# Ending a convolution's last channel block by halves of the tokens, with a norm per half, ahead of a projection in an inference kernel

## The chip, the cores and the metric

The kernel runs on one core of one Trainium2 chip. The metric is the device time of one execution in microseconds (us). The engines named below are PE (TensorE, matrix products), DVE (VectorE), ACT (ScalarE), POOL (GpSimd) and SP (its queue issues the weight loads). Each engine works through its own instructions in the order in which they are written, and waits where one needs something that another engine has not delivered.

## The reference, cut to what matters

Two transformer-like blocks are chained on 512 tokens of 1024 channels. The part that matters is the convolution mixer of the second block, followed by its output projection:

```python
def conformer_conv(h, w_pw1, dw_w, dw_b, ln_g, ln_b, w_pw2):
    a, g = jnp.split(h @ w_pw1, 2, axis=-1)
    u = a * jax.nn.sigmoid(g)
    u = causal_dwconv(u, dw_w, dw_b)          # 31 taps, each channel alone
    u = jax.nn.silu(layer_norm(u, ln_g, ln_b)) # mean and variance over the 1024 channels of a token
    return u @ w_pw2
```

The layer norm needs, for each token, the sum and the sum of squares over all 1024 channels. So nothing of `silu(...)`, and nothing of the projection by `w_pw2`, can start for a token before the convolution of the last channel is done for this token.

## The kernel before, in words

Activations lie with channels on the 128 partitions and the 512 tokens along the free dimension. 1024 channels are 8 blocks (KB = 8), numbered 0 to 7. float32 products are made of three fp32r products: each operand is cut into a high part (names that end in h, or `whi`) and a low part (l, or `wlo`), and high x high, high x low and low x high are added in PSUM.

The order of the work is written out by hand. The program issues instructions engine by engine in the order of the Python code, and waits between engines follow from the tiles that they share. The weights come through one stream `W` in a fixed order: an SP load into a `stage` buffer, an ACT cast to `whi` (line 96), and a DVE subtraction to `wlo` (line 106). Six cut chunks are held, and a slot comes free when PE is done with the chunk in it.

In the convolution stage, for each channel block i, two products of `w_pw1` give `a` and `g`, and `glu` makes u (tile `cu`, with its parts `cuh` and `cul`). The 31 taps are then shared out:
- PE does the first `n_pe[i]` taps as products with a diagonal matrix (`taps`, lines 1628 to 1630, into the PSUM tile `ps_dw`). ACT makes the diagonals `dh` and `dl` (lines 1602 and 1603). A product with the identity adds `pivot`, a rough mean that is taken off for precision (line 1632).
- POOL adds the next `n_pool[i]` taps up in `po`, where ACT does the multiplications.
- DVE does the rest (line 1643), adds the parts, and writes the block's result `y[i]` (lines 1647 to 1649 in `dwconv`).

Two running sums over the blocks (`n1` of y, `n2` of y squared, tiles `acc`) are added up by POOL, and the last but one block's by DVE. ACT makes the squares (tile `term`, line 319), DVE or POOL adds them (line 315). The last block is not added: its y and its square go to the sums over channels as they are.

The sum over channels is a PE product with a column of ones, one column of output per 128 tokens. Such a product appears as two records of shape 128x1 in the trace (in the class `Total`, line 352, tile `ps_ss`; in the class `HalfTotals`, which an earlier stage of the kernel uses, lines 388 and 403, tile `ps_hs`). Then DVE works a chain of some 14 tiny instructions on a few columns, which ends in the reciprocal square root (tile `ry`) and minus the mean times it (`lm`). PE transposes both so that they stand along the tokens on every partition (`turned`, line 443, tile `ps_bc`).

Before the projection each y block is normalised by DVE (lines 1727 and 1728, tile `lt`), put through Silu by ACT and cut into parts (`s0h`, `s0l` and so on). `lead_blocks` runs the first 4 output blocks of the projection abreast (lines 502, 503, 505 and 477 to 479), so that PE has 12 products for each input block as it arrives. The other 4 output blocks follow one at a time, 24 products each (`in_block`). Then the feed-forward part `ffn(1)` starts. Between the small steps `warm(n, ...)` issues products whose result nobody reads (line 458, tile `ps_w`). `S.activation(touch, touch, AF.Silu)` makes ACT load its table for Silu ahead of need.

Of the kernel before, what the change touches and what calls it, by code (L numbers as in the profile page):

```python
# [8 lines left out]
F32 = mybir.dt.float32  # L9
F32R = mybir.dt.float32r  # L10
I32 = mybir.dt.int32
AF = mybir.ActivationFunctionType
# [110 lines left out]
def fused(ctx: ExitStack, tc: tile.TileContext, a, out: bass.AP):  # L123
# [1422 lines left out]
    N_DIAG = 14  # L1546
    n_pe, n_pool = [9] * 6 + [11, 18], [8] * 7 + [7]
# [29 lines left out]
    def glu(i, pa, pg, rb):  # L1577
# [14 lines left out]
        u, w = tap(i, n_pe[i] + n_pool[i])  # L1592
        o2s[i] = bank("o2")
        S.activation(o2s[i], u, AF.Copy, scale=w)
# [22 lines left out]
    def taps(i, k0=0, k1=CW, between=None):  # L1617

        _, uh, ul = cu[i]
        if k0 == 0:  # L1620
            ps_dw[i] = bank("ps_dw")
        ps, n, res = ps_dw[i], n_pe[i], None
        for k in range(k0, min(k1, n)):
            if between and k == k0 + 1:
                res = between()
# [4 lines left out]
            PE.matmul(ps, dl, uh[:, s], start=False, stop=(i < 2 and k == n - 1))  # L1630
        if i > 1 and k1 >= n:
            PE.matmul(ps, identr, pivot, start=False, stop=True)
        return res

    def dwconv(i, k0=0, k1=CW):
# [5 lines left out]
        for m, k in list(enumerate(rest[:-1]))[k0:k1]:  # L1641
            t = ps if m % 2 and i < KB - 1 else o2
            V.scalar_tensor_tensor(t, *tap(i, k), t, op0=ALU.mult, op1=ALU.add)
        if k1 < CW:
            return
# [8 lines left out]
        if 1 < i < KB - 1:  # L1654
            ln_sums(i - 1)
        if i == KB - 1:
            ln_sums(i)


    def ln_sums(i):  # L1660
        last = i == KB - 1
        n1.plain(y[i], last=last)
        n2.square(y[i], last=last)
# [10 lines left out]
    for i in range(KB):  # L1674
# [21 lines left out]
    def begin_sums():  # L1696
        return [Total(n).begin().copy() for n in (n1, n2)]
# [7 lines left out]
    nm = small.tile([P, NT], F32, tag="lm", name="lm")  # L1705
    V.tensor_scalar(nm, s1, -1.0 / D, None, op0=ALU.mult)
    sq = small.tile([P, NT], F32, tag="lq", name="lq")
    V.tensor_scalar(sq, s2, 1.0 / D, EPS, op0=ALU.mult, op1=ALU.add)
    var = small.tile([P, NT], F32, tag="lv", name="lv")
    V.tensor_mul(var, nm, nm)  # L1710
    V.scalar_tensor_tensor(var, var, -1.0, sq, op0=ALU.mult, op1=ALU.add)
# [12 lines left out]
    def ln_a(i):  # L1724
        if i < KB:
            t = work("lt")
            V.tensor_mul(t, y[i], rb)
            V.tensor_add(t, t, nb)
            sl[i] = part_pair(f"s{i}", slp, "sl")
            if i == 0:  # L1730
                S.activation(sl[i][0], t, AF.Silu, bias=col("ln_b", i), scale=col("ln_g", i))
            S.activation(t, t, AF.Silu, bias=col("ln_b", i), scale=col("ln_g", i))
            if i > 0:
                S.copy(sl[i][0], t)
            cur[i] = t

    def ln_b(i):
        ln_a(i + 1)
        return second_part(sl[i], cur.pop(i))

    lead = 4
    ln_a(0)
    pss = lead_blocks(ln_b, lead)
# [104 lines left out]
```

## Time and profile before

| what | us |
|---|---|
| median of 3 runs (lowest, highest) | 1699.74 (1699.52, 1700.22) |
| the profiled execution's own time | 1698.82 |
| span of its trace | 1696.5 |
| PE busy, by the page | 1684.5 |
| first product of the projection by `w_pw2` starts at | 1288.64 |
| first product of `ffn(1)` starts at | 1332.28 |

Times in the trace count from the start of the span. The profiled execution took 2.3 us more than its span, and 0.92 us less than the median of the runs. A busy time counts the length of the records; PE's records overlap, because one product enters the array before the one ahead has left it. So the pace of PE is read from the distance between starts and not from the length of a record.

### The profile page before, as it was taken

The page shows a single profiled execution, that of the slowest core. Times are in us where ns is not written, and L with a number is a line of the kernel's source. Part 1 is how long each engine was busy: PE and PEld are TensorE (multiplying, and loading weights), DVE is VectorE, ACT ScalarE, POOL GpSimd, SP SyncE. Part 2 cuts the span into 40 slices and gives each one's busy share as a digit, 9 for nine tenths or more (in the row PEclk, how much of TensorE's full clock was granted, in tenths as well). Part 3 has the DMA queues.
Part 4 walks back from the last instruction along what each step waited for, and adds up shares of the span by engine and source line. Part 5 has one row for each costly group of instructions (what it writes and reads, how often), then busy time and mean ns, then how long its engine had stood idle before and what let it go on. Part 6 is the DMA issues. An engine that isn't in the chain of part 4 may idle for free.

```text
span 1696.5 us, 20684 instructions
## 1 busy us (share of the span) xinstructions
PE 1684.5 (99%) x7950; PEld 1409.8 (83%) x7950; DVE 1089.1 (64%) x1780; ACT 754.6 (44%) x1237; POOL 109.5 (6%) x104
## 2 busy tenths in 40 slices
PE   9999999999999999999999999999999999999999
PEld 7888898888888987888888888888887888888887
DVE  8877866244346876765874377557987487636752
ACT  4433453333233345863543244457885254323430
POOL 0000000000000000000000000006880000000000
PEclk8999999999999999999999999999999999999999
DMA  9477315332324132112333332232210223333332
GB/s 355 151 235 237 100 60 167 109 96 86 119 66 121 48 107 88 51 32 68 101 95 92 110 100 84 87 115 88 74 51 17 83 88 110 93 109 100 91 99 71
DMA packets 53667, 176.12 MB, mean 104 GB/s; under 512 B 6081, under 2 KB 6337, under 8 KB 52674
## 3 DMA queue, kind: packets, MB, share of 16 engines
q1 hardware_dynamic: 53570, 174.82, 32.0%
q8 instruction: 62, 1.02, 0.3%
q14 instruction: 35, 0.29, 0.1%
HBM read 172.69 MB, written 2.10 MB: 103 GB/s over the span
## 4 chain that ended last, share of the span: by engine, by line
PE 95%; DVE 2%; ACT 1%; issue 0%; DMA 0%; SPq 0%; ACTq 0%; DVEq 0%
PE ps L477 25%; PE ps L478 25%; PE ps L479 25%; PE ps L621 2%; PE ps L1121 1%; PE ps L1123 1%; PE ps L1122 1%; PE ps L502 1%; PE ps L503 1%; PE ps L505 1%; PE ps_dw L1628 1%; PE ps_dw L1629 1%; PE ps_dw L1630 1%; PE ps_ss L352 1%; PE ps L915 1%; PE ps L912 1%
## 5 line engine op out<-in xcount | busy, mean ns | idle before, releaser
L106 DVE TENSOR_TENSOR wlo<-stage,whi 128x1024 fp32r<-128x1024 f32 (+3 forms) x312 | 336.2, 1104 | 82.2 <-ACT whi L96 81.1
L96 ACT CAST whi<-stage 128x1024 fp32r<-128x1024 f32 (+3 forms) x312 | 288.4, 950 | 178.4 <-DMA stage<-in_down 50.4
L1482 ACT ACTIVATE zo<-z,par 128x512 f32<-128x512 f32 x88 | 70.4, 814 | 156.6 <-DVE z L1480 156.5
L1486 DVE SCALAR_TENSOR_TENSOR zo<-z,par,zo 128x510 f32<-128x510 f32 (+1 forms) x176 | 123.4, 746 | 11.0 <-ACT zo L1482 11.0
L1480 DVE TENSOR_TENSOR z<-ps,rbc 128x512 f32<-128x512 f32 x88 | 59.2, 686 | 72.5 <-PE ps L479 69.0
L1575 POOL TENSOR_TENSOR po<-po,pr 128x512 f32<-128x512 f32 x55 | 73.0, 1328 | 18.2 <-ACT pr L1574 14.5
L545 DVE SCALAR_TENSOR_TENSOR ada<-ada,cs 128x1024 f32<-128x1024 f32 x48 | 58.3, 1218 | 7.8 <-DMA ada<-in_ada 7.7
L1489 ACT ACTIVATE zo<-zo 128x512 f32<-128x512 f32 x44 | 27.9, 633 | 66.2 <-DVE zo L1486 66.2
L1527 DVE TENSOR_TENSOR x<-x,ps 128x512 f32<-128x512 f32 x16 | 11.0, 688 | 67.1 <-PE ps L479 67.1
L932 DVE TENSOR_TENSOR r<-r 128x512 f32<-128x512 f32 x32 | 22.1, 690 | 46.6 <-ACT r L930 46.6
L315 DVE TENSOR_TENSOR acc<-acc,term 128x512 f32<-128x512 f32 (+1 forms) x68 | 44.2, 664 | 7.0 <-ACT term L319 5.8
L930 ACT ACTIVATE r<-ps 128x512 f32<-128x512 f32 x32 | 19.0, 595 | 60.4 <-PE ps L479 56.7
L963 DVE TENSOR_TENSOR y<-y,ps 128x512 f32<-128x512 f32 x14 | 9.6, 687 | 48.8 <-PE ps L479 48.8
L477 PE MATMUL ps<-n7h,whi 128*128 128x512 f32 x104 | 40.7, 391 | 0.0
L479 PE MATMUL ps<-n7h,wlo 128*128 128x512 f32 x104 | 40.5, 389 | 0.0
L478 PE MATMUL ps<-n7l,whi 128*128 128x512 f32 x104 | 40.5, 389 | 0.0
L1574 ACT ACTIVATE pr<-cu,par 128x512 f32<-128x512 f32 x55 | 39.0, 713 | 2.8 <-POOL po L1575 2.8
L1416 DVE TENSOR_TENSOR x<-x,ps 128x512 f32<-128x512 f32 x24 | 16.4, 684 | 35.3 <-PE ps L479 35.3
L477 PE MATMUL ps<-n0h,whi 128*128 128x512 f32 x96 | 38.1, 397 | 0.0
L1244 POOL MEMSET qk<- 128x8 f32 x4 | 0.5, 113 | 580.8 <-DVE mt L561 580.8
L477 PE MATMUL ps<-n1h,whi 128*128 128x512 f32 x96 | 37.4, 390 | 0.0
L479 PE MATMUL ps<-n0h,wlo 128*128 128x512 f32 x96 | 37.4, 389 | 0.0
(1382 smaller groups left out, 4973.0 us busy)
## 6 DMA issues: line engine op xcount, KB each, us to landing
stage<-in_up SPq DMA_DIRECT2D x88, 512.0 KB, 3.8
ada<-in_ada SPq DMA_DIRECT2D x34, 512.0 KB, 4.6
stage<-in_mlp_in SPq DMA_DIRECT2D x32, 512.0 KB, 3.9
stage<-in_down SPq DMA_DIRECT2D x32, 384.0 KB, 3.2
stage<-in_pw SPq DMA_DIRECT2D x24, 512.0 KB, 3.8
stage<-in_down SPq DMA_DIRECT2D x32, 320.0 KB, 3.4
stage<-in_mlp_out SPq DMA_DIRECT2D x28, 320.0 KB, 3.3
stage<-in_sc_in SPq DMA_DIRECT2D x16, 512.0 KB, 3.8
```

What stands on the lines that cost most here:

```text
L96: nc.scalar.copy(hi[:, :w], t[:, :w])
L106: self.nc.vector.tensor_sub(lo, t, hi)
L315: self.engine.tensor_add(self.acc[:, s], self.acc[:, s], t)
L477: PE.matmul(ps, hi, act[0], start=first, stop=False)
L478: PE.matmul(ps, hi, act[1], start=False, stop=False)
L479: PE.matmul(ps, lo, act[0], start=False, stop=last)
L545: V.scalar_tensor_tensor(t[:, s], t[:, s], 1.0, cs[:, s], op0=ALU.mult, op1=ALU.mult, accum_out=to)
L1480: V.tensor_mul(z, ps, rb)
L1482: S.activation(o, z, AF.Identity, bias=col(fcb, j), scale=col(fcw, 2 * 2 * FB + j))
L1486: V.scalar_tensor_tensor(o[:, s:], z[:, :T - s], col(fcw, (2 - s) * 2 * FB + j), o[:, s:], op0=ALU.mult, op1=ALU.add)
L1574: S.activation(pr, u, AF.Copy, scale=w)
L1575: G.tensor_add(po[i], po[i], pr)
```

## The change

The last channel block (number 7) ends by halves of the tokens, 256 each (`PARTS`), with its own sums, norm and transposes for each half. The projection's first output blocks, now 5 in place of 4, run over the first half of the tokens for all 8 input blocks and then over the second half.

- PE takes 19 taps of block 7 (18 before), the first 11 (`N_WHOLE`) on all tokens and the other 8 by halves into another PSUM tile, `ps_de`. ACT makes all 19 diagonals ahead. The activation that wrote one tap into the tile `o2` for block 7 is gone; DVE's 4 taps are added in the PSUM tile of the 11 whole taps.
- The sums over channels use `HalfTotals` with two sums; the `Total` of all tokens and its place between the taps are gone.
- `warm` is called with 2 and 6 where it was called with 7, 8 and 8.

```diff
-    n_pe, n_pool = [9] * 6 + [11, 18], [8] * 7 + [7]
+    n_pe, n_pool = [9] * 6 + [11, 19], [8] * 7 + [7]
...
         if i == KB - 1:
-            taps(i, 0, 15)
+            taps(i, N_WHOLE)
+            for k in range(N_DIAG, n_pe[i]):
+                early[i].append(diagonal(i * CW + k))
         if i > 0:
             dwconv(i - 1)
-    dwconv(KB - 1, 0, CW - 2 - n_pe[-1] - n_pool[-1])
...
+    def half_taps(h):
+        _, uh, ul = cu[last]
+        ps = ends[:, PARTS[h]]
+        for k in range(N_WHOLE, n_pe[last]):
+            dh, dl = early[last][k]
+            s = slice(k + h * (T // 2), k + (h + 1) * (T // 2))
+            PE.matmul(ps, dh, uh[:, s], start=(k == N_WHOLE), stop=False)
+            PE.matmul(ps, dh, ul[:, s], start=False, stop=False)
+            PE.matmul(ps, dl, uh[:, s], start=False, stop=False)
+        PE.matmul(ps, identr, pivot[:, PARTS[h]], start=False, stop=True)
...
+    half_taps(0)
+    half_rest(0)
+    half_end(0)
+    S.activation(touch, touch, AF.Silu)
     n1.by(V), n2.by(V)
     ln_sums(KB - 2)
-    sums = taps(KB - 1, 15, CW, begin_sums)
-    S.activation(touch, touch, AF.Silu)
-    dwconv(KB - 1, CW)
-
-    warm(7, acts[0])
-    s1, s2 = [n.last().end() for n in sums]
...
-    r = rsqrt(var, NT, 1.0, "n", eps=False)
-    warm(8, acts[0])
-    rb = turned(r)
-    V.tensor_mul(nm, nm, r)
-    nb = turned(nm)
-    warm(8, acts[0])
+    tots[0].begin()
+    tots[0].copy()
+    for m in range(2):
+        tots[0].last(m)
+    half_taps(1)
+    half_rest(1)
+    tots[1].begin()
+    warm(2, acts[0])
+    rbs = [half_turned(run(half_norm(0), [lambda: None] * 11 + [lambda: half_end(1)]))]
+    for m in range(2):
+        tots[1].last(m)
+    del cu[last]
+    warm(6, acts[0])
...
-    lead = 4
-    ln_a(0)
-    pss = lead_blocks(ln_b, lead)
+    lead = 5
+    ws = [W.take() for _ in range(lead)]
+    pss = [bank() for _ in range(lead)]
+    tots[1].copy()
+    chain, got = half_norm(1), []
...
+    for h in range(2):
+        s = PARTS[h]
+        ln_a(0, h)
+        for k in range(KB):
+            ln_a(k + 1, h)
+            if h == 0:
+                for _ in range(2):
+                    next(steps, None)
+            ln_b(k, h)
+            if h == 0:
+                next(steps, None)
...
+            for w, ps in zip(ws, pss):
+                PE.matmul(ps[:, s], w[0][:, o], hi, start=(k == 0), stop=False)
+                PE.matmul(ps[:, s], w[1][:, o], hi, start=False, stop=False)
+            for w, ps in zip(ws, pss):
+                PE.matmul(ps[:, s], w[0][:, o], lo, start=False, stop=(k == KB - 1))
```

`half_rest(h)` adds POOL's part and the last tap to a half of y on DVE; `half_end(h)` adds `ps_de` (DVE, line 1716 of the changed kernel) and squares the half (ACT); `half_norm(h)` is the chain of tiny DVE instructions for one half; `half_turned` transposes its two results into one tile `ps_bc`.

What moved on the engines is shown at three places, each time before and then changed. The numbers behind names tell tiles apart that the program calls by one name.

First ACT, from the last diagonals of block 7 to the first Silu of the projection. `y_10738` is the result of block 5; block 6 is `y_10992` before and `y_10994` in the change; block 7 is `y_11045` before and `y_11002` in the change.

```order
L319 ACTIVATE term_10997<-y_10738 128x512
L319 ACTIVATE term_11005<-y_10992 128x512 [waits DVE_49]
L1602 ACTIVATE dh_11008<-ident_125,dwh_9462 128x128 [waits PE_49]
...
L1603 ACTIVATE dl_11037<-ident_125,dwl_9463 128x128 [waits PE_49]
L1700 ACT_TABLE_LOAD
L1700 ACTIVATE touch_9468<-touch_9468 128x1
L319 ACTIVATE term_11049<-y_11045 128x512 [waits DVE_49]
```

```order
L1604 ACTIVATE dl_10981<-ident_125,dwl_9463 128x128 [waits PE_49]
L319 ACTIVATE term_10999<-y_10738 128x512
L319 ACTIVATE term_11039<-y_11002 128x256 [waits DVE_49]
L1749 ACT_TABLE_LOAD
L1749 ACTIVATE touch_9468<-touch_9468 128x1
L319 ACTIVATE term_11043<-y_10994 128x512
L319 ACTIVATE term_11112<-y_11002 128x256 [waits DVE_49]
```

Block 6's square moved from a place ahead of the last three pairs of diagonals to one behind all 19 pairs, behind the square of the first half of block 7, and behind the table load.

Second PE, from the last taps to the first product of the projection. `acc_9928` is the running sum of y and `acc_9930` that of the squares; in the change `term_11039` is the square of the first half of block 7.

```order
L352 MATMUL ps_ss_11015<-ones_123,acc_9928 128x1 x4
L352 MATMUL ps_ss_11022<-ones_123,acc_9930 128x1 x4
L1628 MATMUL ps_dw_10932<-cuh_10806,dh_11029 128x512
...
L1632 MATMUL ps_dw_10932<-pivot_9470,identr_134 128x512
L458 MATMUL ps_w_11051<-n0h_9062,identr_134 128x512 x7
L352 MATMUL ps_ss_11015<-ones_123,y_11045 128x1 x4
L352 MATMUL ps_ss_11022<-ones_123,term_11049 128x1 x4
L458 MATMUL ps_w_11090<-n0h_9062,identr_134 128x512 x8
```

```order
L1706 MATMUL ps_de_11006<-pivot_9470,identr_134 128x256
L388 MATMUL ps_hs_11004<-ones_123,acc_9928 128x1 x2
L388 MATMUL ps_hs_11004<-ones_123,acc_9930 128x1 x2
L388 MATMUL ps_hs_11004<-ones_123,y_11002 128x1 x2
L388 MATMUL ps_hs_11004<-ones_123,term_11039 128x1 x2
L1703 MATMUL ps_de_11006<-cuh_10806,dh_10918 128x256
...
L458 MATMUL ps_w_11086<-n0h_9062,identr_134 128x512 x2
L1743 MATMUL ps_bc_11116<-ident_125,ry_11098 128x128 x2
L1743 MATMUL ps_bc_11116<-ident_125,lm_11091 128x128 x2
L388 MATMUL ps_hs_11005<-ones_123,y_11002 128x1 x2
L388 MATMUL ps_hs_11005<-ones_123,term_11112 128x1 x2
L458 MATMUL ps_w_11125<-n0h_9062,identr_134 128x512 x6
```

In the change all of the first half's sums stand between the two halves of the taps, and no `warm` stands there. The sums of the second half's y and square stand behind the transposes of the first half.

Third DVE, from the chain of tiny instructions to the first normalised block, with what each instruction waits for.

```order
L287 TENSOR_TENSOR rt<-rt,rh 128x4
L292 SCALAR_TENSOR_TENSOR ry<-rt,ry 128x4 [waits DVE_49]
L1715 TENSOR_TENSOR lm<-lm,ry 128x4 [waits DVE_49]
L1727 TENSOR_TENSOR lt<-y,ps_bc 128x512 [waits PE_49]
L1728 TENSOR_TENSOR lt<-lt,ps_bc 128x512 [waits DVE_49,PE_49]
```

```order
L287 TENSOR_TENSOR rt<-rt,rh 128x2
L1716 TENSOR_TENSOR y<-y,ps_de 128x256 [waits PE_49]
L292 SCALAR_TENSOR_TENSOR ry<-rt,ry 128x2 [waits DVE_49]
L1735 TENSOR_TENSOR lm<-lm,ry 128x2 [waits DVE_49]
L395 COPY lns<-ps_hs 128x2x2 [waits PE_49]
L1776 TENSOR_TENSOR lt<-y,ps_bc 128x256
L1777 TENSOR_TENSOR lt<-lt,ps_bc 128x256 [waits DVE_49]
```

The addition that ends the second half of y now stands inside the first half's chain, and a copy of the second half's sums stands ahead of the first `lt`. It is the copy that waits for PE, and the `lt` behind it waits for PE no more.

## Rows read from the trace of the kernel before

**Rows 1.** The page: busy time, share of the span and instructions of each engine.

```profile
PE 1684.5 (99%) x7950; PEld 1409.8 (83%) x7950; DVE 1089.1 (64%) x1780; ACT 754.6 (44%) x1237; POOL 109.5 (6%) x104
```

**Rows 2.** Timeline of PE: start, length, operation, count, [idle before, releaser].

```profile
1275.91 1.95 PE L352 MATMUL ps_ss<-ones,acc 128*128 128x1 f32 x16 [0.55 <-DVE acc L315]
...
1285.97 0.60 PE L443 MATMUL ps_bc<-ident,lm 128*128 128x128 f32 x4
...
1288.64 0.50 PE L502 MATMUL ps<-s0h,whi 128*128 128x512 f32 x1 [0.19 <-ACT s0h L1731]
```

**Rows 3.** Timeline of DVE over the same stretch.

```profile
1272.14 3.12 DVE L1643 SCALAR_TENSOR_TENSOR o<-cu,par,o 128x512 f32<-128x512 f32 x4
...
1275.77 0.69 DVE L315 TENSOR_TENSOR acc<-acc,term 128x512 f32<-128x512 f32 x1
...
1282.94 0.16 DVE L368 TENSOR_TENSOR tot<-tot,ps_ss 128x4 f32<-128x4 f32 x1 [0.74 <-PE ps_ss L352]
...
1285.08 0.15 DVE L287 TENSOR_TENSOR rt<-rt,rh 128x4 f32<-128x4 f32 x1
```

**Rows 4.** Timeline of ACT over the same stretch.

```profile
1275.42 0.39 ACT L1603 ACTIVATE dl<-ident,dwl 128x128 fp32r<-128x128 f32 x1
1275.84 1.28 ACT L1700 ACT_TABLE_LOAD   x1
1277.13 0.20 ACT L1700 ACTIVATE touch<-touch 128x1 f32<-128x1 f32 x1
1280.35 0.64 ACT L319 ACTIVATE term<-y 128x512 f32<-128x512 f32 x1 [3.02 <-DVE y L1649]
```

**Rows 5.** Timelines of an earlier stage and its 256-token instructions, DVE and ACT.

```profile
551.46 0.41 DVE L988 TENSOR_TENSOR y<-y,ps 128x256 f32<-128x256 f32 x1
...
551.97 0.42 ACT L319 ACTIVATE term<-y 128x256 f32<-128x256 f32 x1 [3.95 <-DVE y L988]
...
552.76 0.48 DVE L329 SCALAR_TENSOR_TENSOR term<-y,gate,x 128x256 f32<-128x256 f32 x1
...
197.41 0.60 ACT L816 ACTIVATE a0h<-mt,mod,scale 128x256 fp32r<-128x256 f32 x1 [0.82 <-DVE mt L561]
```

**Rows 6.** Timelines of PE: four output blocks of 24, the next stage's first, 256-token products.

```profile
1310.52 0.39 PE L477 MATMUL ps<-s0h,whi 128*128 128x512 f32 x1
...
1332.28 0.39 PE L502 MATMUL ps<-n0h,whi 128*128 128x512 f32 x1
...
1685.26 0.28 PE L477 MATMUL ps<-f11h,whi 128*128 128x256 f32 x1
...
1693.05 0.28 PE L479 MATMUL ps<-f21h,wlo 128*128 128x256 f32 x1
```

**Rows 7.** Windows: busy times (instructions), granted clock, DMA share, GB/s.

```profile
564.00:568.00 4.00, 3.03 (x19) 2.86 (x19) 3.78 (x14) 2.10 (x5) 0.00 (x0) 0.80 0.01 4
568.00:572.00 4.00, 4.00 (x19) 3.96 (x19) 3.93 (x15) 1.66 (x4) 0.00 (x0) 0.50 0.00 0
572.00:576.00 4.00, 4.00 (x32) 4.00 (x31) 3.14 (x14) 1.22 (x3) 0.00 (x0) 0.85 0.02 4
1274.00:1278.00 4.00, 3.45 (x23) 2.76 (x22) 2.69 (x7) 3.30 (x9) 0.91 (x1) 1.00 0.01 4
```

**Rows 8.** Timeline of PE around the first of these windows.

```profile
563.04 1.40 PE L388 MATMUL ps_hs<-ones,acc 128*128 128x1 f32 x12
565.41 0.39 PE L1099 MATMUL ps<-e0h,whi 128*128 128x256 f32 x1 [0.97 <-ACT e0h L1028]
...
566.94 0.41 PE L1100 MATMUL ps<-e1h,wlo 128*128 128x256 f32 x1
...
567.79 0.41 PE L1100 MATMUL ps<-e1h,wlo 128*128 128x256 f32 x1
...
568.85 0.85 PE L388 MATMUL ps_hs<-ones,term 128*128 128x1 f32 x4
569.55 0.56 PE L1099 MATMUL ps<-e2h,whi 128*128 128x256 f32 x1
```

More of the change, by code (lines that the diff above doesn't have):

```diff
@@ L1615, in prepare, with taps @@
                 pool_tap(i, k + j)
-    def taps(i, k0=0, k1=CW, between=None):
+    def taps(i, k1=CW):
         _, uh, ul = cu[i]
[L1620 to L1625, printed above, removed]
+        ps_dw[i] = bank("ps_dw")
+        ps, n = ps_dw[i], n_pe[i]
+        for k in range(min(k1, n)):
             dh, dl = early[i][k] if k < N_DIAG else diagonal(i * CW + k)
@@ L1640, in dwconv @@
         rest = list(range(n + 1, CW))
-        for m, k in list(enumerate(rest[:-1]))[k0:k1]:
-            t = ps if m % 2 and i < KB - 1 else o2
+        for m, k in enumerate(rest[:-1]):
+            t = ps if m % 2 else o2
             V.scalar_tensor_tensor(t, *tap(i, k), t, op0=ALU.mult, op1=ALU.add)
-        if k1 < CW:
-            return
         o = yp.tile([P, 8 * DA], F32, tag="y", name="y")[:, :T]
@@ L1653, in dwconv @@
             V.tensor_add(o, o, pivot.bitcast(F32))
[L1654 removed]
+        if i > 1:
             ln_sums(i - 1)
[L1656 to L1657 removed]
     def ln_sums(i):
[L1661 to L1663 removed]
+        n1.plain(y[i])
+        n2.square(y[i])
     def make_pivot():
@@ L1688, in fused @@
         if i == KB - 1:
-            taps(i, 0, 15)
+            taps(i, N_WHOLE)
+            for k in range(N_DIAG, n_pe[i]):
+                early[i].append(diagonal(i * CW + k))
         if i > 0:
             dwconv(i - 1)
-    dwconv(KB - 1, 0, CW - 2 - n_pe[-1] - n_pool[-1])
+    last, n = KB - 1, n_pe[-1] + n_pool[-1]
+    y[last] = yp.tile([P, 8 * DA], F32, tag="y", name="y")[:, :T]
+    lnsums = small.tile([P, 2, NT], F32, tag="lns", name="lns", bufs=1)
+    tots = [HalfTotals((n1, n2), h, lnsums) for h in range(2)]
@@ new lines, in fused @@
+    H = NT // 2
+    whole, ends = ps_dw[last], bank("ps_de")
+    for k in range(n, CW - 1):
+        V.scalar_tensor_tensor(whole, *tap(last, k), whole, op0=ALU.mult, op1=ALU.add)
+    def half_taps(h):
[8 more added lines that the diff above has]
+        PE.matmul(ps, identr, pivot[:, PARTS[h]], start=False, stop=True)
@@ new lines, in half_rest, with half_end, half_norm @@
+    def half_rest(h):
+        s = PARTS[h]
+        u, w = tap(last, CW - 1)
+        V.tensor_add(whole[:, s], whole[:, s], po[last][:, s])
+        V.scalar_tensor_tensor(y[last][:, s], u[:, s], w, whole[:, s], op0=ALU.mult, op1=ALU.add)
+    def half_end(h):
+        s = PARTS[h]
+        V.tensor_add(y[last][:, s], y[last][:, s], ends[:, s])
+        n1.last = y[last][:, s]
+        n2.square(y[last][:, s], last=True, s=s)
+    def half_norm(h):
+        t = tots[h]
+        s1, s2 = t.end(0), t.end(1)
+        yield
+        nm, sq, var = (small.tile([P, H], F32, tag=f"l{h}{m}", name=m, bufs=1) for m in ("lm", "lq", "lv"))
+        V.tensor_scalar(nm, s1, -1.0 / D, None, op0=ALU.mult)
+        V.tensor_scalar(sq, s2, 1.0 / D, EPS, op0=ALU.mult, op1=ALU.add)
+        yield
+        V.tensor_mul(var, nm, nm)
+        yield
+        V.scalar_tensor_tensor(var, var, -1.0, sq, op0=ALU.mult, op1=ALU.add)
+        yield
+        r = yield from rsqrt_steps(var, H, 1.0, "n", eps=False)
+        yield
+        V.tensor_mul(nm, nm, r)
+        return r, nm
@@ L1693, in fused, with half_turned @@
+    def half_turned(pair):
+        ps = bank("ps_bc")
+        for i, r in enumerate(pair):
+            for j in range(H):
+                o = (i * H + j) * P
+                PE.transpose(ps[:, o:o + P], r[:, j:j + 1].to_broadcast([P, P]), ident)
+        return ps[:, :T // 2], ps[:, T // 2:]
+    half_taps(0)
+    half_rest(0)
+    half_end(0)
+    S.activation(touch, touch, AF.Silu)
     n1.by(V), n2.by(V)
     ln_sums(KB - 2)
-    def begin_sums():
-        return [Total(n).begin().copy() for n in (n1, n2)]
```

54 lines of the change are left out of this document (30 added, 24 removed).

## Prediction

> **What bounds the kernel now.** I read the page first: PE is busy for 1684.5 us, 99% [rows 1]. So time can be won only where PE's records are work that nobody reads, or tiny, and it is lost where PE gets more to do or waits. Then I read the timelines of PE, DVE and ACT around the end of the convolution, to see what PE does between the last taps and the first product of the projection. PE sums the two running sums at 1275.91, after 0.55 us of idling for DVE, and the projection starts at 1288.64, released by ACT's first Silu [rows 2]. The reader is to see a chain with PE as filler: the last of y, its square, the sums over channels, tiny DVE instructions, transposes, normalising, Silu. The change wants to run a half's chain beside the other half's taps. From 1288.64 to 1332.28, where `ffn(1)` starts, PE is dense: 43.64 us for 192 products [rows 2, 6]. What the change is worth is therefore read from two numbers: when the projection starts, and how long it takes.
>
> **The change step by step: the first half's sums.** Block 6's result is written before 1272.14, where DVE starts four taps of block 7, and four such taps take 3.12 us [rows 3]. They need the 11 whole taps, 5 taps fewer than PE has done before the sums at 1275.91; 5 x 3 products at 0.23 us are 3.5 us, so these are ready when DVE comes. Half 0 then costs DVE an addition, a multiply-add and the addition of `ps_de`: 0.41 + 0.48 + 0.41, the lengths of 256-token instructions [rows 5]. y's first half is there at 1272.14 + 3.12 + 1.3 = 1276.6. PE is done with the first half of the eight taps by about 1275.2: 25 products of 0.12, behind ACT's diagonals, of which the last before ended at 1275.81 [rows 4]; the change adds a pair, but takes a square pair and the `o2` activation from ahead of them.
>
> Now ACT. It squares the half, 0.42 [rows 5], to 1277.1; loads its table, 1.28, to 1278.4; runs `touch`, 0.20, to 1278.6; and only then squares block 6, 0.64, to 1279.2 [rows 4]. Before, block 6's square was done long before the load. DVE adds it to the running sum in 0.69 [rows 3], to 1279.9. PE has no instruction that it may run meanwhile: the sum of `acc` stands ahead of the second half of the taps in its order. Then come 4 tiny records, a DVE copy of 0.16 that the next ones wait for, and 8 more tiny records. 16 take 1.95 [rows 2], 0.12 each, so the second half of the taps starts at 1279.9 + 0.7 + 0.2 + 1.0 = 1281.8. From 1275.2 to there PE idles or runs tiny records, 6.6 us, without a `warm`.
>
> The load starts 0.03 us after the last diagonal's end, and the next activation 0.01 us after the load [rows 4], so I count the load alone. The Trainium skill (ScalarE: Activation LUTs, section What ACT_TABLE_LOAD costs) says that a switch costs a drain of about 1.38 us besides the load; by an estimate from it the sum would be 1.4 us higher.
>
> **The clock.** The trace shows what such a pause can do. At 563.04 PE ran 12 tiny records and idled to 565.41, and from there dense products [rows 8]. The granted clock then shows 0.80, 0.50 and 0.85 of full in three windows of 4 us [rows 7], which is the lower level (1.2 GHz) for about 1.6 + 4.0 + 1.2 = 6.8 us. Against it, 16 tiny records and 0.55 of idling near 1276 left it at 1.00 [rows 2, 7]. 6.6 us is far more than either, so I take it that the clock falls before the second half of the taps. Four products of 256 columns then take 0.85, 0.21 each [rows 8], against 7.79 / 65 = 0.12 at full clock [rows 6]; four tiny records take 0.70 [rows 8], 0.17 each. Twelve tiny ones cost 0.7 more, and the taps start at 1282.5. All 25 at the lower clock are 5.3 us; with the last few at full clock again about 4.8. Call the end 1287.5 (1285.0 with no fall: 1281.8 + 3.0 + 0.2; 1288.0 with none at full clock).
>
> **From there to the projection.** Half 1 of y is added inside the first half's chain (0.41), and two tiny DVE steps follow. The rest of that chain, 1285.08 - 1282.94 = 2.1 before [rows 3], is hidden by the taps; its cover gone, it would end at about 1284.2. PE has, in order: 8 tiny records (1.0, of which 0.8 lie behind the end of the taps), 2 `warm` (0.45), 4 transposes (0.60 [rows 2]), 8 tiny records for the second half (0.95). DVE's copy of these sums waits for the last of them, and the first `lt` is queued behind it, though it needs only the first half: 0.2. Two additions that follow each other, 0.85; Silu 0.60 [rows 5], the length of a 256-token activation with scale and bias; 0.06 to PE. That is 0.8 + 0.45 + 0.6 + 0.95 + 0.2 + 0.85 + 0.66 = 4.5 us at full clock, 6 at the lower one (the products 1.5 more). I take 4.5, as the taps have been dense by then: the projection starts at 1287.5 + 4.5 = 1292.0, **3.4 us later** than before.
>
> **The projection.** Five blocks by halves are 2 x 5 x 24 = 240 products of 0.1198, 28.75; four transposes of the second half stand among them, 0.35; three blocks of 24 whole products at (1332.28 - 1310.52) / 96 = 0.2267 are 16.32 [rows 6]. Together 45.4 against 43.64: **1.8 us longer**. PE needs 15 x 0.12 = 1.8 us for an input block in a half; DVE needs three 256-token instructions, about 1.2, and up to three tiny steps of 0.2, so it keeps up, and the second norm's chain is done before PE comes to its transposes. The weights are cut at the same places in the order; after the fifth block DVE works through residuals at 3 us a block, but `ffn(1)` needs the last of them only at its eighth input block, some 19 us later, so this costs nothing; without that cover it would be up to 3 us.
>
> Of the 1.8, the halving itself is 1.55: 2 x 0.1198 - 0.2267 = 0.013 us for each of 120 whole products [rows 6]. The Trainium skill (TensorE: Matmul & The Clock Gate, section Back-to-back issue gap) gives N / 2.4 + 2.5 ns for a product of N columns at full clock. By an estimate from it the halving costs 2.5 ns for each, 0.3 us in all, and the sum would be 1.25 lower.
>
> **Sum.** 3.4 + 1.8 = 5.2 us. The profiled execution's 1698.82 becomes 1704.0; the runs' median of 1699.74 lies 0.92 above it, so 1704.9.
>
> **Rivals.**
> *The clock doesn't fall.* The taps end at 1285.0, the projection starts at 1289.5: +0.9, and 1.8 for the projection: +2.7, 1702.4. For it: near 1276 it didn't fall. Against: that pause was less than half as long. 0.16.
>
> *The lower clock reaches into the projection.* The tiny stretch behind the taps is 1.5 longer and some 3 us of the projection run at half pace, 1.5 more: +8.2 with the sum, 1707.9. For it: between 565.41 and 573.2 dense products ran at the lower clock for most of 6.8 us, and tiny ones stood among them [rows 7, 8], as they do here. 0.26.
>
> *Block 6's square is not late.* If ACT got to it before the table load, DVE's addition would follow its first one at 1277.2 and end at 1277.9, PE would start the second half at 1279.8 and end it at 1283.0; + 4.5 is 1287.5, 1.1 earlier than before; with the projection's 1.8 longer that is +0.7, 1700.4, not slower by what can be told. It decides if that addition starts before about 1278. For it: ACT's busy times are low and its table is needed 8 us later; against: the order puts the square behind the load, and ACT doesn't overtake. 0.05. To come out faster by 0.2% the projection would have to start 5.2 us earlier than now; 0.03 for what I don't see.
>
> **How the numbers follow.** The forecast has 0.50. 0.2% is 3.4 us, about what a measurement of this kernel can tell from no change. Slower by more: nine tenths of the forecast's share, since its own range is 3.2 to 6.5 (the taps' end 1285.9 to 1288.0, the tail 4.5 to 5.3), and all of the second rival: 0.45 + 0.26 = 0.71, with a little of the first 0.73. Within: the rest of the forecast, most of the first rival and of the third, 0.23. Faster: 0.04. The range takes in the first rival and most of the second: 1702.0 to 1708.2; the forecast's own is 1702.9 to 1706.2.
>
> **What would show it.** In the changed trace: ACT's table load between the half's square and block 6's, and PE idle, released by DVE's addition to `acc`, until about 1279.9; the granted clock near 0.5 somewhere in 1279 to 1287 and 256-token taps 0.21 apart; the copy of the sums ahead of the first `lt`, released by PE; the first product of the projection near 1292 and `ffn(1)`'s near 1337.4. I am wrong if PE starts the second half of the taps before 1280, if the first `lt` starts before the second half's sums, or if stalls of the projection move `ffn(1)` by more than the sum.

## The result and the profile after

The changed kernel took 1717.0 us (median of 4 runs, 1715.95 to 1720.72) where the kernel before took 1699.63 (4 runs, 1698.47 to 1700.22): a ratio of 1.010, with an interval of 1.0086 to 1.0114. It is slower, as forecast, but by 17.4 us and not by 5.2, and outside the forecast's range of 1702.0 to 1708.2. The span of the profiled execution grew from 1696.5 to 1713.8 us, by 17.3.

The page, set beside [rows 1], shows PE busy for 12.8 us more, with 133 more records.

```profile
PE 1697.3 (99%) x8083; PEld 1415.9 (83%) x8083; DVE 1094.6 (64%) x1825; ACT 759.2 (44%) x1255; POOL 109.9 (6%) x104
```

To see where the 17.3 us went, I cut the trace at places that both kernels have. The timeline of PE (after), the counterpart of [rows 2, 6], has the last block's first tap, the end of the first half's taps, the sums, the second half's taps from first to last, the projection's first product, and the first product of `ffn(1)`.

```profile
1272.20 0.40 PE L1626 MATMUL ps_dw<-cuh,dh 128*128 128x512 f32 x1
...
1283.34 0.27 PE L1706 MATMUL ps_de<-pivot,identr 128*128 128x256 f32 x1
1285.81 1.01 PE L388 MATMUL ps_hs<-ones,acc 128*128 128x1 f32 x4 [2.20 <-DVE acc L315]
1288.48 1.01 PE L388 MATMUL ps_hs<-ones,acc 128*128 128x1 f32 x4 [1.67 <-DVE acc L315]
1289.75 1.01 PE L388 MATMUL ps_hs<-ones,y 128*128 128x1 f32 x4 [0.25 <-DVE lns L395]
...
1291.48 0.56 PE L1703 MATMUL ps_de<-cuh,dh 128*128 128x256 f32 x1
...
1296.39 0.28 PE L1706 MATMUL ps_de<-pivot,identr 128*128 128x256 f32 x1
...
1301.01 0.38 PE L1819 MATMUL ps<-s0h,whi 128*128 128x256 f32 x1 [0.25 <-ACT s0h L1782]
...
1346.35 0.39 PE L502 MATMUL ps<-n0h,whi 128*128 128x512 f32 x1
```

The same first tap stands at 1263.89 in the trace before:

```profile
1263.89 0.39 PE L1628 MATMUL ps_dw<-cuh,dh 128*128 128x512 f32 x1
```

| stretch | before | after | more |
|---|---|---|---|
| start to the last block's first tap | 1263.89 | 1272.20 | 8.31 |
| from there to the projection's first product | 24.75 | 28.81 | 4.06 |
| the projection, to the first product of `ffn(1)` | 43.64 | 45.34 | 1.70 |
| from there to the last product's start | 360.77 | 363.93 | 3.16 |

The changed products of PE lie in the second and third stretch, which take 5.76 us more, against 5.2 forecast. The other 11.47 us were lost where PE's products are the same in both kernels (6011 records ahead of the last block's first tap in either trace). Windows of PE alone (length, busy and records, granted clock, DMA share, GB/s) show how. First the kernel before in three stretches of a hidden layer's products, then the changed one:

```profile
420.00:440.00 20.00, 20.00 (x90) 1.00 0.40 125
440.00:460.00 20.00, 20.00 (x90) 1.00 0.42 133
...
1500.00:1520.00 20.00, 20.00 (x90) 1.00 0.34 110
```

```profile
420.00:440.00 20.00, 20.00 (x88) 1.00 0.31 98
440.00:460.00 20.00, 20.00 (x87) 1.00 0.41 132
...
1500.00:1520.00 20.00, 20.00 (x87) 1.00 0.25 77
```

PE is busy all the time and the clock is granted in full in both, but in 20 us it starts 87 or 88 products and not 90. It isn't waiting; each product is longer. By the starts of some 1,720 products that follow each other in the hidden layers (tiles `h` and `f`) one comes every 0.2267 us before and every 0.2333 after; some 3,700 of the normalised inputs (`a` and `n`) come every 0.2268 in both. 1,720 x 0.0066 is 11.4 us. Each trace holds one execution, and a stretch varies between executions: in `a_fit`, `b_256` and `b_512` (below), whose products keep the pace of the kernel before, the last block's first tap stands at 1263.35, 1266.41 and 1267.46. So the pace of the products is the surer reading, and the stretches agree with it.

What differs for `h` and `f` is where they stand. The change allocates one more small tile, `lnsums`, of 32 bytes on each partition, in the pool `small`. The pools of the stages (hidden layers, gates, convolution, normalised blocks) follow `small` in SBUF, the memory in which all these tiles stand, so every tile in them starts 32 bytes further on. No trace prints an address. But with each tile rounded up to 32 bytes, the tiles that the kernel allocates in `small` add up to 4096 bytes before and to 4128 after, and the pools between the weights' buffers and `small` hold only tiles of 2048 and 4096 bytes. So by this count a hidden layer and its weights `whi` and `wlo` start alike within 2048 bytes before, and 32 bytes apart after. The normalised inputs stand ahead of `small`, as the weights do, and start like them in both kernels.

### The profile page after: what moved, and what is told of

Its sections match the earlier page's. It is cut to its first block, busy times and chain, and to the rows that moved or that the text cites. A ratio compares the mean times of both kernels' runs of the same rounds, so it can differ in the third digit from the quotient of the medians.

```text
span 1713.8 us, 21016 instructions
## 1 busy us (share of the span) xinstructions
PE 1697.3 (99%) x8083; PEld 1415.9 (83%) x8083; DVE 1094.6 (64%) x1825; ACT 759.2 (44%) x1255; POOL 109.9 (6%) x104
## 4 chain that ended last, share of the span: by engine, by line
PE 95%; DVE 3%; ACT 2%; DMA 0%; issue 0%; SPq 0%; ACTq 0%; DVEq 0%
PE ps L477 25%; PE ps L478 25%; PE ps L479 25%; PE ps L621 2%; PE ps L1121 1%; PE ps L1123 1%; PE ps L1122 1%; PE ps_dw L1628 1%; PE ps_dw L1627 1%; PE ps_dw L1626 1%; PE ps L503 1%; PE ps L502 1%; PE ps L505 1%; PE ps L915 1%; PE ps L1819 1%; PE ps L1820 1%
## 5 line engine op out<-in xcount | busy, mean ns | idle before, releaser
L479 PE MATMUL ps<-n1h,wlo 128*128 128x512 f32 x96 | 37.4, 390 | 0.0
```

What stands on the lines that cost most here:

```text
L479: PE.matmul(ps, lo, act[0], start=False, stop=last)
```

## Experiments: the address

**Does the place of these tiles cost the 11 us?** The pool `small` begins with a tile that nobody uses, so its length (`LINE` is 32 float32, 128 bytes; 8 more are 32 bytes) moves every pool behind it, with no other edit. `a_line` is the changed kernel, `b_32` and `b_64` are the kernel before:

```
-    small.tile([P, LINE], F32, name="pad", bufs=1)
+    small.tile([P, LINE + 8], F32, name="pad", bufs=1)     # a_line, b_32
+    small.tile([P, LINE + 16], F32, name="pad", bufs=1)    # b_64
```

> The changed kernel, with the unused tile at the head of the pool of small tiles made 32 bytes longer, so that every tile of the pools behind it starts 64 bytes from where it stood in the kernel before, instead of 32. No instruction is added. Address theory: products of 512 columns whose moving operand lies in one of those pools (hidden layers, gates, normalised blocks) come every 0.2267 us again instead of every 0.2334; some 1,920 of them at 0.0067 are 12.9 us, so 1717.0 becomes about 1704.1 (1703 to 1706), which is the forecast's 1704.9 within its range. Rival, the new work itself or a state of the chip makes the products of the hidden layers slower: 1717, with 0.2334 as before.

> The kernel before with the same unused tile 32 bytes longer, and nothing else. Address theory: hidden-layer products come every 0.2334 us, all 192 products of the second projection too; some 2,040 at 0.0067, 13.7 us, so 1699.6 becomes about 1713 (1711 to 1715). Rival, the slower products belong to the changed instructions: 1699.6, within 1 us.

> The kernel before with the unused tile 64 bytes longer. If what counts is the start within 64 bytes, 1699.6 within 1 us and 0.2267 a product. If any move of these tiles costs, or the start within 128 bytes counts, about 1713 as with 32.

The kernel before took 1701.31 us beside these. `b_32` took 1715.75 (1.0080, 1.0064 to 1.0097): 32 unused bytes, and no instruction of the change, cost 14.4 us (11 to 15 were expected). Not all of that need be the address: in the profiled execution of `b_32` the clock fell at the end of the convolution, which took 3.1 us more by it (the last section has this). The stretches whose products slowed make some 12.7: 8.31 and 3.16 as in the table above, and 1.27 in the projection. In windows of `b_32`, hidden layers first, normalised inputs last, only the hidden layers are slower:

```profile
420.00:440.00 20.00, 20.00 (x87) 1.00 0.26 82
...
1420.00:1440.00 20.00, 20.00 (x90) 1.00 0.31 108
```

The two kernels that stand 64 bytes off fell between the two answers: `a_line` 1710.24 (1.0045, 1.0027 to 1.0062) and `b_64` 1704.65 (1.0019, 1.0009 to 1.0029), and in both a product of the hidden layers comes every 0.2290 us. So the address bears on the length, but my first rule, that the start within 64 bytes counts, fell.

**Within 128 bytes?** `a_96` makes the tile of the changed kernel 96 bytes longer (`LINE + 24`), so the stages' tiles start 128 bytes from where they stand before.

> The changed kernel with the unused tile 96 bytes longer: every tile of the pools behind it starts 128 bytes from where it stood in the kernel before. Address theory, now with the start within 128 bytes: all hidden-layer products back at 0.2267 us, where 64 bytes gave about 0.229 on the mean and 32 bytes 0.2334. The time is that of the forecast, 1704.9 (1703 to 1706.5) where the kernel before shows 1699.6, a ratio of 1.003; ffn(1) starts 73.6 us after the last block's first tap, against 68.4 before. Rival, what is left of the loss with 64 bytes is not the address: 0.229 and some 1709 again.

1716.74 us against 1699.78 (1.0094, 1.0077 to 1.0110), and as slow as with 32 bytes:

```profile
420.00:440.00 20.00, 20.00 (x88) 1.00 0.28 88
440.00:460.00 20.00, 20.00 (x87) 1.00 0.42 142
```

That rule fell too. By the count above, a product's moving tile (the activations, named first behind `<-` in a row) and its weights start alike in the kernel before. So the next theory was the distance between the two tiles that one product reads. `a_fit` shortens the changed kernel's unused tile by the 32 bytes that `lnsums` adds (`LINE - 8`); `b_w32` moves the weights instead; `b_512` and `b_256` lengthen the tile of the kernel before (`LINE + 128`, `LINE + 64`).

```
     wsp = ctx.enter_context(tc.tile_pool(name="wsp", bufs=1))
+    wsp.tile([P, 8], F32, name="shift", bufs=1)            # b_w32
```

> The changed kernel with the unused tile 32 bytes shorter, so that every tile of the pools behind it stands exactly where it stands in the kernel before. Address theory (what counts is where a product's moving tile stands against its weights): hidden-layer products back at 0.2267 us and the time at the forecast, 1704.9 (1703 to 1706.5). Rival, the slower products belong to the changed kernel: 0.2334 and 1717.

> The kernel before with 32 unused bytes ahead of the weights' buffers: the weights and every pool behind them move by 32 bytes, the pool of the normalised inputs, which stands ahead of them, stays. Relative theory (the distance from the moving tile to its weights counts): hidden-layer products stay at 0.2267, as both moved, and the products of the normalised inputs, some 3,700, come every 0.2334: 25 us more, about 1725. Rival, the start of the moving tile by itself counts: the hidden layers at 0.2334, the normalised inputs at 0.2267, about 1713.

> The kernel before with the unused tile 512 bytes longer. The moving tile and its weights then stand alike within 512 bytes, as in the kernel before, but not within 2048. If 512 bytes are the period of whatever collides: 1699.6 and 0.2267. If the period is longer: hidden layers at 0.23 or more, 1708 to 1714.

> The kernel before with the unused tile 256 bytes longer. If the period is 256 bytes or a divisor of it that 128 isn't: 0.2267 a product and 1699.6 to 1701. If it is 512: the hidden layers at 0.229 to 0.2334, 1704 to 1714.

`a_fit` took 1704.51 us against 1699.96 (1.0030, 1.0021 to 1.0039), beside the forecast's 1704.9. `b_w32` took 1726.84 (1.0155, 1.0140 to 1.0171). Its windows are those of `b_32` turned round: the hidden layers, which moved together with the weights, are at 90 products, and the normalised inputs, which didn't move, are slow. So the start of the moving tile by itself doesn't count. (In `b_w32` the pool `wk`, which stands right behind the weights, moved with them; that the distance counts from the weights and not from a tile of `wk` is taken from this, that a product reads no tile of `wk`.)

```profile
440.00:460.00 20.00, 20.00 (x90) 1.00 0.45 147
...
1420.00:1440.00 20.00, 20.00 (x87) 1.00 0.32 106
```

`b_512` (1702.65, 1.0007, 0.9997 to 1.0017) and `b_256` (1701.18, 0.9997, 0.9987 to 1.0006) are the kernel before again, in time and in pace. All ten kernels, by the mean distance in us between starts in their traces:

| moving tile against weights, bytes | kernel | hidden layers (some 1,720) | normalised inputs (some 3,700) |
|---|---|---|---|
| 0 for both | before, `a_fit` | 0.2267 | 0.2268 |
| +32 for hidden layers | after, `b_32` | 0.2333 | 0.2268 |
| +64 for hidden layers | `a_line`, `b_64` | 0.2290 | 0.2269 |
| +128 for hidden layers | `a_96` | 0.2333 | 0.2268 |
| +256, +512 for hidden layers | `b_256`, `b_512` | 0.2267 | 0.2268 |
| -32 for normalised inputs | `b_w32` | 0.2268 | 0.2333 |

The rival that the new instructions make the products slow would have left `a_fit` at 1717 and `b_32` at 1699.6; the one came out 12 us lower and the other 14 us slower than its base. What inside the chip makes a product at such a distance longer isn't shown by a trace; 32 and 128 bytes are slow, 64 is between, 0, 256 and 512 aren't. Other distances weren't tried.

This holds for 512 columns. The few products of 256 columns on hidden layers (65 on tiles `f`) go another way: one comes every 0.1199 us at 0, 256 and 512 bytes, 0.1185 at 128, 0.1178 at 64 and 0.1167 at 32. For them the distance of the kernel before is the slowest.

## Experiments: the end of the convolution

With the addresses apart, the changed lines themselves cost some 5 us. The next runs take their steps apart. Three of them (`a_96_warm`, `a_96_sq`, `a_best`) stand on the slow address of `a_96`, so they are compared with `a_96` by the time from the last block's first tap to the projection's first product (29.03 us in `a_96`; 28.42 to 28.86 in the three other kernels with this order, `a_line`, `after` and `a_fit`). Each of these stretches is read from one execution.

**Without PE's pause, and without the late square.** `a_96_warm` gives PE unread products in its pauses. `a_96_sq` lets ACT square block 6 ahead of the table load:

```
-    tots[0].begin()                                        # a_96_warm
+    warm(9, acts[0])
+    for m, s in enumerate((n1, n2)):
+        tots[0]._products(s.acc, 0, m, 0)                  # the small records of one running sum
+        if m == 0:
+            warm(7, acts[0])
...
+    n1.by(V), n2.by(V)                                     # a_96_sq
+    six = n2.square(y[KB - 2], later=True)
     half_end(0)
     S.activation(touch, touch, AF.Silu)
-    n1.by(V), n2.by(V)
-    ln_sums(KB - 2)
+    n1.plain(y[KB - 2])
+    six()
```

> As a_96, and PE is given 9 products of 512 columns that nobody reads ahead of the first half's sums and 7 between the sums of the two running sums, so that it doesn't idle there; no wait is removed. Clock theory: the granted clock stays at full, the second half's taps take 3.0 us instead of 4.9 and the small records behind them less, so the projection starts 2 to 3 us earlier than in a_96 and the time is 2 to 3 us less, near 1702.5. Rival, the pause isn't what the clock falls for, or it falls in the tail instead: within 1 us of a_96.

> As a_96, and ACT squares block 6 ahead of the half's square and the table load; PE's order is as in the change. Theory: the sums start 1.9 us earlier (the load, the touch and the order of the squares no longer stand in the way), and the pause of PE ahead of the second half's taps is some 2.4 us instead of 4; the projection starts 1.9 us earlier if the clock still falls (1703), 4 to 5 us earlier if it now holds (1700.5). Rival, block 6's square is hidden and something else makes the sums late: as a_96.

Times: 1714.19 (1.0082, 1.0066 to 1.0099) and 1715.0 (1.0098, 1.0069 to 1.0127); by time alone neither can be told from `a_96`. The traces can: the stretch is 27.13 us with the unread products, 1.90 shorter where 2 to 3 were expected, and 25.06 with the early square, 3.97 shorter, between the 1.9 expected with a fall of the clock and the 4 to 5 without. In `a_96_warm` the granted clock stays at full through the former pause and falls only behind the last 12 small records, which have waits of 0.34 and 0.26 us ahead of them and among them (windows of PE; the taps of the second half start at 1289.51):

```profile
1286.00:1288.00 2.00, 1.66 (x9) 1.00 0.00 0
1288.00:1290.00 2.00, 1.75 (x16) 1.00 0.00 0
1290.00:1292.00 2.00, 2.00 (x13) 0.64 0.00 0
1292.00:1294.00 2.00, 2.00 (x11) 0.51 0.00 0
```

So filling the pause moved the fall of the clock and shortened it, and didn't do away with it. In `a_96_sq` the products of both running sums follow each other with no second pause, as the theory had it; its clock still falls behind them (0.50 from 1290 to 1292):

```profile
1287.13 1.21 PE L388 MATMUL ps_hs<-ones,acc 128*128 128x1 f32 x8 [2.21 <-DVE acc L315]
1288.60 0.61 PE L388 MATMUL ps_hs<-ones,y 128*128 128x1 f32 x4 [0.26 <-DVE lns L395]
...
1289.58 0.56 PE L1703 MATMUL ps_de<-cuh,dh 128*128 128x256 f32 x1
```

**Taps ahead of the sums.** `a_both` (on the address of `a_line`) has the early square, and the second half's taps issued ahead of the first half's sums:

```
+    half_taps(1)
     tots[0].begin()
...
-    half_taps(1)
     half_rest(1)
```

> The changed kernel with the 32 bytes, and two moves in its order: ACT squares block 6 ahead of the half's square and the table load, and PE is given the second half's taps ahead of the first half's sums. Theory of the prediction (PE idles because block 6's square stands behind the load and the taps behind the sums; the clock falls in that pause): the taps run on without a pause and end about 3 us after the first half's; the first half's sums, 11 small DVE steps, transposes, normalising and Silu follow, so the projection starts some 5 us earlier than in the changed kernel with the 32 bytes alone: 1699 (1697.5 to 1701.5). Rival, the clock falls all the same in the tail behind the taps (small records and idling for DVE): the projection starts only some 2 us earlier and runs its first products at half pace, 1702 to 1703.5.

1709.61 us beside 1710.24 of `a_line`, and the projection starts 1.99 us earlier: the rival was nearer. Two rows of PE show that the taps didn't run on. The second half's first tap waits 1.57 us for DVE, which reads the first half from the same tile in PSUM, `ps_de`:

```profile
1280.16 0.28 PE L1706 MATMUL ps_de<-pivot,identr 128*128 128x256 f32 x1
...
1282.02 0.38 PE L1703 MATMUL ps_de<-cuh,dh 128*128 128x256 f32 x1 [1.57 <-DVE y L1716]
```

The projection starts 26.43 us after the first tap (28.42 in `a_line`), but the clock has now fallen behind the small records and is still down when it starts, at 1295.44, so it takes 46.51 us and not 45.30:

```profile
1292.00:1294.00 2.00, 2.00 (x8) 0.50 0.00 0
1294.00:1296.00 2.00, 2.00 (x7) 0.50 0.00 0
1296.00:1298.00 2.00, 2.00 (x11) 0.50 0.00 0
```

**Can the change pay?** The question is whether the changed order can beat the kernel before once its losses are mended. `a_best` takes the early square, fills the pause, and moves the second half's sums behind the first norm's transposes and their copy behind two normalised blocks. `a_best2` does so on the addresses of `a_fit`, with unread products between the groups of small records and the last sums behind the projection's first input block; `a_best3` has them behind the second. The cut leaves out the early square and the steps of the second norm, which start one or two input blocks later in `a_best2` and `a_best3`.

```
+    warm(10, acts[0])
     tots[0].begin()
+    warm(3, acts[0])                                       # not in a_best
     tots[0].copy()
...
-    tots[1].begin()
-    warm(2, acts[0])
     rbs = [half_turned(run(half_norm(0), [lambda: None] * 11 + [lambda: half_end(1)]))]
-    for m in range(2):                                     # stays in a_best, behind begin()
-        tots[1].last(m)
+    warm(2, acts[0])                                       # not in a_best
+    tots[1].begin()
     del cu[last]
-    warm(6, acts[0])
...
-    tots[1].copy()                                         # a_best: behind two normalised blocks
...
+            if h == 0 and k == 0:                          # a_best2; k == 1 in a_best3
+                tots[1].copy()
+                for m in range(2):
+                    tots[1].last(m)
```

> As a_96_sq, with 10 unread products of 512 columns in PE's pause, the second half's sums moved behind the transposes of the first half's norm (where the change has them ahead, with two unread products), the copy of these sums on DVE moved behind the first two normalised blocks, and the six unread products ahead of the projection left out. Theory: with the clock at full the projection starts about 21.5 us after the last block's first tap, against 24.75 in the kernel before, and takes 45.2 us against 43.64: ffn(1) starts 1.7 us earlier than in the kernel before, 1698 (1697 to 1699). Rival, the clock falls at the 16 small records behind the taps: the first 3 to 7 us of the projection at half pace, 1700 to 1702.

> The kernel of a_fit, with ACT squaring block 6 ahead of the half's square, 10 unread products of 512 columns ahead of the first half's sums and 3 between their two groups, the second half's sums over the earlier blocks behind the first norm's transposes and two unread products, and its last sums and their copy behind the first input block of the projection. Theory: the small records no longer stand 16 in a row, so the clock holds; the projection starts 21 to 21.5 us after the last block's first tap, where the kernel before has 24.75, and takes 45.2 us against 43.64: 1698 (1697 to 1699.5). Rival, the clock falls behind the first group of sums all the same: the second half's taps at half pace, 1.9 us more, 1700 to 1701.

> As a_best2, with the second half's last sums and their copy behind the second input block of the projection instead of the first, and its norm's steps one input block later. Theory: DVE no longer waits for these sums between two input blocks, so the projection takes 45.2 to 45.7 us instead of 46.5, ffn(1) starts 67.7 to 68.1 us after the last block's first tap against 68.4 in the kernel before, and the time is that of the kernel before less at most 0.7: no change that can be told. Rival, the wait only moves by an input block: 46.5 again.

`a_best`: 1713.91 against 1699.78 (1.0080, 1.0064 to 1.0097), on the slow address; its projection starts after 23.43 us but takes 47.34. The clock fell twice: to 0.50 behind the first half's sums, over the last of the second half's taps, and to 0.60 and 0.55 from 1296 to 1300, behind the 16 small records that follow the taps. The projection had begun at 1295.54, so its first products ran at half pace: the rival. `a_best2`: 1702.1 against 1699.96 (1.0007, 0.9997 to 1.0016). `a_best3`: 1700.9 against 1701.34 (1.0008, 0.9998 to 1.0018). In both the granted clock is 1.00 in every window of this stretch, as their theory had it, and the projection starts 22.40 us after the first tap, 2.35 earlier than in the kernel before. It takes 46.53 us, 2.9 more, and there the gain goes: `ffn(1)` starts 68.93 us after the first tap, against 68.39. Of the 2.9, 2.0 are the price of the projection by halves, as `a_fit` has it (45.66); the rest are the 8 small records of the last sums, 0.80 us, which stand inside the projection in both and which my 45.2 us had left out (the rival of `a_best3`). The timeline of PE in `a_best3`:

```profile
1285.95 0.38 PE L1820 MATMUL ps<-s0h,whi 128*128 128x256 f32 x1 [0.42 <-ACT s0h L1783]
...
1289.64 0.50 PE L388 MATMUL ps_hs<-ones,y 128*128 128x1 f32 x4
1290.00 0.58 PE L388 MATMUL ps_hs<-ones,term 128*128 128x1 f32 x4
1290.44 0.36 PE L1820 MATMUL ps<-s2h,whi 128*128 128x256 f32 x1
```

No version was faster than the kernel before by what can be told.

## Why the prediction was wrong

**The step that failed** is the sum: "3.4 + 1.8 = 5.2 us". Its two terms are those of the changed lines, and it takes all the rest of the kernel as it was, at nothing and without a reason. The change's tiles were never costed for where they put the others: `lnsums` moved the stages' pools by 32 bytes against the weights, and the hidden layers' products, which no step of mine touched, lost 0.0066 us each. Most of the 17.3 us is that: 11.47 outside the changed stretches. `a_fit`, which takes only this away, lies 4.55 us above the kernel before by the medians, near the forecast's 5.2. Some of that is luck: by its trace the two changed stretches take 6.1 us more, 4.1 and 2.0, and the rest of that execution 0.5 less. No rival held it either; the 0.03 "for what I don't see" stood on the faster side alone. The trace before may have hinted at it: a tap of 512 columns, whose moving tile starts k elements further on, came slower than a projection's product. I took 0.23 for one and 0.2267 for the other without asking why; that the address makes this difference too isn't shown.

**The other steps, in order.** *ACT's order* was right. The half's square, the load, the touch and block 6's square follow each other as forecast (timeline of ACT, after):

```profile
1285.18 0.42 ACT L319 ACTIVATE term<-y 128x256 f32<-128x256 f32 x1 [1.60 <-DVE y L1716]
1285.62 1.28 ACT L1749 ACT_TABLE_LOAD   x1
1286.91 0.20 ACT L1749 ACTIVATE touch<-touch 128x1 f32<-128x1 f32 x1
1287.02 0.61 ACT L319 ACTIVATE term<-y 128x512 f32<-128x512 f32 x1
```

The last ends 15.43 us after the block's first tap, where 1279.2 was 15.3. The load stands 0.02 us behind the square and the touch 0.01 behind the load. The Trainium skill (ScalarE: Activation LUTs, section What ACT_TABLE_LOAD costs) has a drain of about 1.38 us besides the load; no run here shows one, and the sum without it came out within 0.1 us.

*The clock* fell where forecast, in the pause: windows of PE (after).

```profile
1284.00:1286.00 2.00, 0.19 (x1) 0.92 0.04 8
1286.00:1288.00 2.00, 0.82 (x4) 0.50 0.00 0
...
1294.00:1296.00 2.00, 2.00 (x11) 0.52 0.00 0
1296.00:1298.00 2.00, 2.00 (x18) 1.00 0.00 0
```

All 16 small records ran at the lower level, where I had slowed 12, and four of them waited 0.25 us for DVE's copy; so the second half's taps start 19.28 us after the first tap and not 18.6, and end at 24.31 (forecast 23.6). This is the 0.7 by which the projection starts late: 4.06 and not 3.4. But the row that I set against a fall, 16 records and 0.55 of idling that left the clock at 1.00, was one execution of an order that goes both ways (last section): where it falls, the kernel before takes 26.31 us to the projection, and the change costs 2.5 us there. *The tail* is 4.50 us from the taps' end, as summed, and the first `lt` does stand behind the copy that waits for PE (timeline of DVE, after, the counterpart of [rows 3]):

```profile
1299.30 0.16 DVE L395 COPY lns<-ps_hs 128x4 f32<-128x4 f32 x1 [1.90 <-PE ps_hs L388]
1299.38 0.41 DVE L1776 TENSOR_TENSOR lt<-y,ps_bc 128x256 f32<-128x256 f32 x1
```

*The projection* took 45.34 us against 45.4, by two errors that met: its three whole blocks came every 0.233 us, and its 240 products of 256 columns every 0.117, below the 0.1198 of [rows 6]. On the old addresses (`a_fit`) it took 45.66, with 0.1199 each, so there the halving costs 2 x 0.1199 - 0.2267 = 0.013 a product, as the rows had it; at 32 bytes it costs next to nothing, 2 x 0.1167 - 0.2333 = 0.0001. The Trainium skill (TensorE: Matmul & The Clock Gate, section Back-to-back issue gap) gives N / 2.4 + 2.5 ns for the gap of a product by itself; by an estimate from it the halving costs 0.0025. Neither measured value agrees with that, and the measurement decides.

*The rivals.* "The clock doesn't fall": in none of the changed orders but `a_best2` and `a_best3`, which break up the small records. "The lower clock reaches into the projection": not after the change, where it is back at 1296, but in `a_both` and `a_best`. "Block 6's square is not late": it was, and `a_96_sq` shows its price, 3.97 us with a shorter fall of the clock; the rival had the projection 4.5 us ahead of the forecast, with no fall.

## What to carry to other kernels

Before an edit is costed, compare where the two programs put every tile: one small tile in a shared pool moved all pools behind it by 32 bytes, and a 3% loss in the products of untouched stages came to twice the price of the edit. Where products of 512 columns are PE's bound, try moving tiles and weights that start 0, 256 or 512 bytes apart, by an unused tile if need be, and measure: products of 256 columns here came fastest at 32. A loss of this kind shows in a trace as fewer products in a window of full PE and full clock. And an engine that works in order needs something that it may run ahead of every wait: the early square for ACT and unread products among the small records of PE brought back what the new order had lost here, though no more than that.

## What the runs showed of the hardware

- With PE dense and the clock at full, a product of 512 columns came every 0.2267 us where its moving tile and its weights start 0, 256 or 512 bytes apart, every 0.2290 at 64, and every 0.2333 at 32 and 128. The distances are those of the edits, counted from the kernel before.
- The products of 256 columns go the other way: 0.1167 us at 32 bytes in the changed kernel against 0.1199 at 0 in `a_fit`.
- Small records close together brought the granted clock to about 0.5 behind them, with dense products ahead: 16 with a wait of 0.26 us among them in `a_best`, 12 with waits of 0.34 and 0.26 in `a_96_warm`. With 3 unread products between two groups of 8, which also filled that wait, it stayed at 1.00 in the one execution each of `a_best2` and `a_best3`; which of the two keeps it up isn't shown.
- In the kernel before, 16 such records after a wait of 0.55 us left the clock at 1.00 [rows 2, 7]. But six kernels have this order there, and the profiled executions split: it stayed at 1.00 in `before`, `b_256` and `b_64`, and fell to 0.5 behind the records in `b_512`, `b_w32` and `b_32`, after waits of 0.51 to 0.55 in all six. Windows behind the records, before (all engines, as in [rows 7]) and then `b_512` (PE alone):

```profile
1278.00:1282.00 4.00, 4.00 (x24) 3.38 (x22) 2.10 (x4) 0.64 (x1) 0.00 (x0) 1.00 0.00 0
```

```profile
1280.00:1282.00 2.00, 2.00 (x15) 0.81 0.04 8
1282.00:1284.00 2.00, 2.00 (x6) 0.50 0.00 0
```

  From the last block's first tap to the projection the first three took 24.75 us each, the others 26.31, 26.31 and 27.87. So the order of before stands close to the fall, and its median may well mix the two; what share of its executions falls isn't shown. `a_best3`, with `ffn(1)` 68.93 us after the first tap, stands between the 68.39 of before and the 69.96 of `b_512`.
- PE's next product into the PSUM tile `ps_de` waited 1.57 us until DVE had read the other half of the tile (`a_both`). Waits here follow from shared tiles; whether the chip needs this one isn't shown.
